# A hybrid attention block on one core: forget gates' sums by a recurrence on VectorE, projection products placed between a linear head's levels, other queue orders at the two norms

## The chip, the core and the metric

The kernel runs on one core of one Trainium2 chip. Five engines work side by side, each through its own queue in order: TensorE (PE, matrix products and transpositions), VectorE (DVE), ScalarE (ACT, activation functions and copies), GpSimd (POOL) and SyncE (SP, which here only issues transfers). Waits between them go by semaphores. The metric is the device time of one execution in microseconds (us); the time before is a median of 937.77 us over three runs, 936.5 to 938.24.

## What is computed

One layer over 512 tokens of width 1024, with 16 learned meta tokens ahead of them (T = 528) that are dropped at the end. The input is normed and projected to all parts; a stick-breaking attention (8 heads of 64) and a gated linear attention (GLA, 4 heads, key width 128, value width 256) run on the same normed tokens; sigmoid gates merge them, `w_o` projects back, and after a second norm a gated MLP (width 2816) with a causal convolution follows. The change lies mostly in the linear attention and in the two norms. Cut to that, the reference is:

```python
h = rmsnorm(concat([meta, x]), norm_mix_pre)
... = split(h @ w_in)                        # sb q,k,v; gla q,k,v; r; lr (16 wide); gates
g = log_sigmoid(lr @ w_gk_up + b_gk) / 16    # log forget gate, per token and key channel
# GLA, per head, S: 128 x 256
S_t = diag(exp(g_t)) S_{t-1} + k_t^T v_t
o_t = q_t S_t
gla = rmsnorm_per_head(o) * silu(r)
```

The kernel works in chunks of 128 tokens. With `cum` the running sum of g inside a chunk, a pair of tokens t > s in one chunk has the weight (q_t exp(cum_t)) . (k_s exp(-cum_s)). So that no exponential overflows, the pairs are dealt out to levels 64, 32, 16, 8, 4, 2 and 1: at level l, block after block of 2l tokens, the later half is taken against the earlier, with `cum` counted from the last token of the earlier half.

## The kernel before

Numbers are float32. A product is made as three products in the faster type fp32r: an operand is split into a high part (a cast on ACT) and a low part (a subtraction on DVE or POOL), and high x high, high x low and low x high are added in PSUM.

**Weights.** `load_w` (L78 to L91) fetches a block of 128 columns as `raw_x` by a transfer that SP issues, casts it to `wh_x` on ACT (L88) and subtracts on POOL (or DVE) to `wl_x` (L89). There are three raw buffers and two of each part. In the names, gk, gq, gv, gr are the linear heads' key, query, value and output gate, sk, sq, sv the attention's, mg and ms the merging gates', ga and up the MLP's.

**Projections.** `proj` (L100, products at L115) makes `pt_x` (128 columns x 528 tokens, or 514 for gr): for each of eight input blocks three products, each over two segments of tokens (272 and 256), 48 products in all. It issues them in one go; where they land on TensorE is chosen by the scheduler, which orders each engine's queue from the order of the program and its own estimates of time, with `tc.issue_after` as a means to hold an instruction behind another.

**First norm** (L214 to L300). Tokens come as four tiles of 128 (`xt`) and the meta tokens (`xm`). Each is squared and summed on ACT, scaled, transposed on TensorE (`tp`, `tpm`), multiplied by the gain on DVE (`yg`, `ygm`, L210), and split into `hnh` (ACT, L211) and `hnl` (DVE or POOL, L212). TensorE's first projection products, `pt_gk` of head 0 over the first 272 tokens, need tiles 1 and 2 and the meta tokens.

**Forget gates** (L367 to L409). The low-rank projection `lr` (16 wide) is made for all tokens, then for each chunk one product `pg` (L402) gives 128 tokens x 512 channels. The bias, spread over 128 partitions by its own transfer (`bbc`), is added on DVE, and Abs, Exp and Ln on ACT give the log sigmoid in `G`, tokens on the partitions.

**A linear head** (`gla`, L436). It is called for four heads. First five fp32 products of `G` with a triangle of 1/16, `ucum`, sum the gates and turn them (`cum`, L440: 10 rows in the profile), and ACT copies the result. Then come the near blocks of 32 (`dg`, L451), the factors of each level on DVE and ACT (`factors`, L458), the levels' small products (`pl`, L482 for 64 and 32, L493 for 16 to 1), the transposed values (`vt`, L520) and keys (`kdt`, L541), and the recurrence over chunks (`po` L558, `pu` L565, with splits of the state on DVE). The output is normed, transposed (`ot`, L590), multiplied by the gate that two gr projections give, and split into `oh` and `ol` (L142, L143). The main loop then makes the next head's projections:

```python
kqv = gla_proj(0)
for h in range(GH):
    gla(h, *kqv)
    kqv = gla_proj(h + 1) if h + 1 < GH else sb_proj(0)
```

All projections of gr and of the next head are thus free work that the scheduler places where TensorE would wait.

**End of the last linear head.** `sb_proj(0)` (L336) makes the first pair of attention heads; `sb_parts` (L612) splits keys and queries into `ks`, `qh` and `ql` on ACT and DVE, transposes the values (`svt`), and the logits of the 16 meta tokens (`zs`, L640) are the first products that need them. The second pair's projections (`pt_sk`, `pt_sq`) and then the merging gates' (mg) follow as free work; with two buffers, `wh_mg` takes the one that the products of `pt_sq` leave.

**Second norm** (L863 to L1010). `w_o`'s products, then per tile of 128 tokens: `hb` (residual), a square on ACT (`wk`, L883), the root (`r_ffn`, Ln at L124 and Exp at L125), `y` on DVE (L888), a transposition (`ht`, L897), and the split into `h2h` and `h2l`. The first products of the MLP (`pt_up`, `ga`) fill in between tiles 3 and 4; `wh_ga` are two blocks of its weights.

Of the kernel before, what the change touches and what calls it, by code (L numbers as in the profile page):

```python
# [39 lines left out]
C_MSB, C_MGLA = 4624, 5648  # L40
CHUNKS = [(0, 128), (128, 128), (256, 128), (384, 128), (512, 16)]
WARM = 6
EASY = 4
EARLY = 3
# [5 lines left out]
def block_kernel(ctx: ExitStack, tc: tile.TileContext, x, meta_tokens, norm_mix_pre, w_in, w_gk_up, b_gk,  # L50
# [22 lines left out]
    def f32(ap):  # L73
        return ap.bitcast(F32)
# [4 lines left out]
    def load_w(src, nk, name, hi_out=None, lo_out=None, lo_eng=pool, into=None):  # L79
# [8 lines left out]
        act.copy(hi_out, raw)  # L88
        lo_eng.tensor_tensor(out=lo_out, in0=raw, in1=f32(hi_out), op=ALU.subtract)  # L89
# [10 lines left out]
    def proj(w, xh, xl, segs, name, apart=False, only=None, pt=None, by_part=False):  # L100
# [11 lines left out]
        for grp in ([[s] for s in segs] if apart else [segs]):  # L112
            for n, (k, a, b) in enumerate(steps):
                for dst, lo, hi in grp:
                    last_pr[0] = pe.matmul(dst, a[:, k, :], b[:, k, lo:hi], start=n == 0, stop=n == len(steps) - 1)  # L115
        return pt if begins else pt[:m, 512 - l1 + l0 : 512 + l2 - l1]

    last_exp = [None]

    def rstd_of(pl, ss, n, name, between=None, rest=None):  # L120
# [15 lines left out]
        dve.scalar_tensor_tensor(out=a, in0=a, scalar=1.5, in1=r0, op0=ALU.add, op1=ALU.mult)  # L136
# [3 lines left out]

    def split(hi, lo, src):
        act.copy(hi, src)  # L142
        last_low[0] = dve.tensor_tensor(out=lo, in0=src, in1=f32(hi), op=ALU.subtract)  # L143
# [36 lines left out]
    ucum = cst.tile([P, P], F32, name="ucum")  # L180
# [6 lines left out]
    pool.memset(ucum, 1.0 / 16.0)  # L187
    pool.affine_select(out=ucum, in_=ucum, compare_op=ALU.is_ge, fill=0.0, base=0, pattern=[[1, P]], channel_multiplier=-1)
# [12 lines left out]
    g2T = cst.tile([P, KT], F32, name="g2T")  # L201
    mT = cst.tile([P, NM - T0, KT], F32, name="mT")
# [4 lines left out]
    def split_g(pl, hi, lo, src, g, nm, lo_eng=dve):  # L207
# [3 lines left out]
        last_hi[0] = act.copy(hi, y)  # L211
        return lo_eng.tensor_tensor(out=lo, in0=y, in1=f32(hi), op=ALU.subtract)  # L212

    with tc.tile_pool(name="p0", bufs=2, side="right") as p0:  # L214
# [37 lines left out]
        def scaled(xt, r, eng):  # L252

            if eng is act:
                act.mul(xt, xt, r)
            else:
                eng.tensor_scalar(out=xt, in0=xt, scalar1=r, scalar2=None, op0=ALU.mult)

        def turned(i, r):
            if not i:  # L260
                tp = pst("tpm")
                last_tp[0] = pe.transpose(tp[:, :P], xm, ident)
                split_g(p0, hnh[:, :, :NM], hnl[:, :, :NM], tp[:, :P].rearrange("p (t k) -> p k t", k=KT), gT, "m")
                return
            t = slice(NM + (i - 1) * P, NM + i * P)
            for b in range(2):
                scaled(xts[i][:, 512 * b : 512 * b + 512], r, SC[i][b])
            for b in range(2):
                tp = pst(f"tp{i}_{b}", "sz"[i % 2])
                for k in range(4):  # L270
                    c = (4 * b + k) * P
                    with tc.issue_after(last_pr[0].ins) if i > 2 else ExitStack():
                        last_tp[0] = pe.transpose(tp[:, k * P : (k + 1) * P], xts[i][:, c : c + P], ident)
                ks = slice(4 * b, 4 * b + 4)
                low = split_g(p0, hnh[:, ks, t], hnl[:, ks, t], tp.rearrange("p (k t) -> p k t", k=4), gT[:, ks], f"{i}_{b}", LO[i][b])
            return low
# [3 lines left out]
        LO = {1: (pool, pool), 2: (dve, pool), 3: (dve, pool), 4: (dve, pool)}  # L280
        d1 = stats(1)
        d2 = stats(2, last_exp[0])
        turned(1, d1)
# [9 lines left out]
        turned(0, d0)  # L293
        hi2 = last_hi[0]
# [5 lines left out]
        turned(3, d3)  # L300
        low4 = turned(4, d4)
# [960 lines left out]
```

## Time and profile before

| | |
|---|---|
| three runs, median | 937.77 us (936.5 to 938.24) |
| the profiled execution's own time | 938.61 us |
| its span in the trace | 936.9 us |
| TensorE busy | 915.9 us, 98% |
| VectorE, ScalarE, GpSimd busy | 621.9, 494.2 and 355.6 us |
| mean rate of the transfers | 100 GB/s |

The span is the time between the first and the last instruction of one profiled execution. The columns of a timeline row are start, duration (both in us), engine, line, operation, the tiles written and read, and in brackets the idle time ahead of it and what ended that. A row of the chain of waits is start, duration, engine and line, and the number of instructions. A row of the windows gives the stretch, its length, the busy time of TensorE, its weight loads, DVE, ACT and POOL, then the clock granted to TensorE (1.00 is full), the transfers' share and their rate.

### The profile page before, as it was taken

What the parts mean: (1) busy time and instruction counts of PE and PEld (TensorE: products, weight loads), DVE (VectorE), ACT (ScalarE), POOL (GpSimd) and SP (SyncE); (2) the same over time, 40 slices, a digit from 0 to 9 for tenths busy, and PEclk for the clock granted to TensorE, in tenths of its full rate; (3) what the DMA queues carried; (4) which work ended last, traced back from release to release, by engine and by line L of the source; (5) the groups of instructions that cost most, each with busy time, mean ns of one, the idle gap of its engine ahead of it and who ended that gap; (6) DMA issues with size and microseconds to landing.
All of it is one profiled execution on the core that took longest, in us unless ns stands there. A gap on an engine that the chain in (4) does not pass through costs nothing.

```text
span 936.9 us, 17749 instructions
## 1 busy us (share of the span) xinstructions
PE 915.9 (98%) x7156; PEld 839.4 (90%) x7156; DVE 621.9 (66%) x1072; ACT 494.2 (53%) x938; POOL 355.6 (38%) x259
## 2 busy tenths in 40 slices
PE   7999999999999999999999998999999999999997
PEld 7999999999999998989998687999999999988885
DVE  6585858686559786888647357455554444578997
ACT  7674747575567665766754245433333333355654
POOL 6533332323355453555545322544444444200200
PEclk9999999999999999999999998999999999999999
DMA  7222222222222222222224542333333333264933
GB/s 203 66 70 75 63 68 69 69 69 69 69 68 69 68 66 72 68 69 68 57 79 127 211 135 90 108 96 91 90 91 90 93 100 100 91 232 184 239 113 131
DMA packets 129875, 93.38 MB, mean 100 GB/s; under 512 B 4080, under 2 KB 114930, under 8 KB 129794
## 3 DMA queue, kind: packets, MB, share of 16 engines
q1 hardware_dynamic: 126178, 82.55, 29.6%
q10 hardware_dynamic: 2112, 6.82, 1.9%
q0 software_dynamic: 1504, 2.88, 1.8%
q8 instruction: 56, 0.92, 0.4%
q14 instruction: 25, 0.20, 0.1%
HBM read 88.05 MB, written 4.19 MB: 98 GB/s over the span
## 4 chain that ended last, share of the span: by engine, by line
PE 94%; DVE 2%; ACT 2%; issue 1%; DMA 0%; POOL 0%; DVEq 0%; POOLq 0%; ACTq 0%
PE pt_up L115 14%; PE ga L936 13%; PE pt_gr L115 5%; PE pt_gv L115 5%; PE pt_mg L115 5%; PE pt_ms L115 5%; PE pt_go L115 5%; PE dA L1108 3%; PE dB L1108 3%; PE dD L1108 3%; PE pt_sv L115 3%; PE pt_gk L115 3%; PE pt_so L115 3%; PE wob L951 3%; PE pt_sk L115 3%; PE pt_gq L115 2%
## 5 line engine op out<-in xcount | busy, mean ns | idle before, releaser
L89 POOL TENSOR_TENSOR wl_up<-raw_up,wh_up 128x1024 fp32r<-128x1024 f32 x22 | 52.9, 2407 | 82.4 <-ACT wh_up L88 82.4
L89 POOL TENSOR_TENSOR wl_ga<-raw_ga,wh_ga 128x1024 fp32r<-128x1024 f32 x22 | 55.3, 2518 | 74.8 <-ACT wh_ga L88 57.5
L115 PE MATMUL pt_up<-h2h,wh_up 128*128 128x256 f32 (+1 forms) x352 | 74.7, 287 | 1.3 <-ACT h2h L142 1.3
L115 PE MATMUL pt_up<-h2l,wh_up 128*128 128x256 f32 (+1 forms) x352 | 74.6, 286 | 0.0
L115 PE MATMUL pt_up<-h2h,wl_up 128*128 128x256 f32 (+1 forms) x352 | 74.4, 285 | 0.0
L936 PE MATMUL ga<-h2h,wh_ga 128*128 128x512 f32 (+1 forms) x192 | 72.5, 377 | 0.0
L936 PE MATMUL ga<-h2h,wl_ga 128*128 128x512 f32 (+1 forms) x192 | 72.3, 377 | 0.0
L936 PE MATMUL ga<-h2l,wh_ga 128*128 128x512 f32 (+1 forms) x192 | 72.3, 377 | 0.0
L88 ACT CAST wh_up<-raw_up 128x1024 fp32r<-128x1024 f32 x22 | 23.1, 1049 | 79.3 <-PE pt_up L115 76.4
L115 PEld LDWEIGHTS pt_up<-h2h,wh_up 128*128 128x128 f32 x352 | 58.0, 193 | 3.5 <-ACT h2h L142 1.8
L115 PEld LDWEIGHTS pt_up<-h2l,wh_up 128*128 128x128 f32 x352 | 56.6, 193 | 0.0
L115 PEld LDWEIGHTS pt_up<-h2h,wl_up 128*128 128x128 f32 x352 | 56.5, 192 | 0.0
L936 PEld LDWEIGHTS ga<-h2h,wl_ga 128*128 128x128 f32 x192 | 36.4, 190 | 7.0
L936 PEld LDWEIGHTS ga<-h2h,wh_ga 128*128 128x128 f32 x192 | 36.7, 191 | 6.1
L936 PEld LDWEIGHTS ga<-h2l,wh_ga 128*128 128x128 f32 x192 | 36.4, 190 | 6.2
L1039 DVE SCALAR_TENSOR_TENSOR cy<-pt_up,cw,cy 128x511 f32<-128x511 f32 (+1 forms) x22 | 16.4, 745 | 36.7 <-ACT cy L1036 36.7
L88 ACT CAST wh_ga<-raw_ga 128x1024 fp32r<-128x1024 f32 x22 | 23.1, 1048 | 26.8 <-PE ga L936 25.6
L1039 DVE SCALAR_TENSOR_TENSOR yp<-pt_up,cw,yp 128x511 f32<-128x511 f32 (+1 forms) x22 | 16.4, 745 | 30.9 <-ACT yp L1036 30.9
L1136 POOL DMA_DIRECT2D tv<-in_w_ffn_down_dram x6 | 7.0, 1172 | 68.4 <-DVE wl_p L143 68.4
L89 POOL TENSOR_TENSOR wl_gr<-raw_gr,wh_gr 128x1024 fp32r<-128x1024 f32 x8 | 19.1, 2385 | 31.0 <-ACT wh_gr L88 29.5
L142 ACT CAST sh_p<-As 128x512 fp32r<-128x512 f32 (+1 forms) x30 | 17.3, 584 | 23.9 <-PE dB L1108 9.6
L115 PE MATMUL pt_gr<-hnh,wh_gr 128*128 128x258 f32 (+1 forms) x128 | 28.2, 294 | 0.0
(574 smaller groups left out, 3140.9 us busy)
## 6 DMA issues: line engine op xcount, KB each, us to landing
raw_up<-in_w_ffn_up_dram SPq DMA_DIRECT2D x22, 512.0 KB, 3.9
raw_ga<-in_w_ffn_gate_dram SPq DMA_DIRECT2D x22, 512.0 KB, 3.8
raw_t<-in_w_ffn_down_dram SPq DMA_DIRECT2D x10, 512.0 KB, 7.4
raw_gv<-in_w_in_dram SPq DMA_DIRECT2D x8, 512.0 KB, 3.9
raw_gr<-in_w_in_dram SPq DMA_DIRECT2D x8, 512.0 KB, 3.8
raw_mg<-in_w_in_dram SPq DMA_DIRECT2D x8, 512.0 KB, 3.9
raw_go<-in_w_gla_out_dram SPq DMA_DIRECT2D x8, 512.0 KB, 4.2
raw_ms<-in_w_in_dram SPq DMA_DIRECT2D x8, 512.0 KB, 3.8
```

The source lines that it names most:

```text
L88: act.copy(hi_out, raw)
L89: lo_eng.tensor_tensor(out=lo_out, in0=raw, in1=f32(hi_out), op=ALU.subtract)
L115: last_pr[0] = pe.matmul(dst, a[:, k, :], b[:, k, lo:hi], start=n == 0, stop=n == len(steps) - 1)
L142: act.copy(hi, src)
L936: last_mm[0] = pe.matmul(pt[:, lo:hi], a[:, k, :], b[:, k, lo:hi], start=lo == 0 and k == 0 and q == 0, stop=k == KT - 1 and q == 2, skip_ ...
L951: last_mm[0] = pe.matmul(pt, a, b, start=q == 0, stop=q == len(ops) - 1)
L1039: dve.scalar_tensor_tensor(out=y[:, d:], in0=pt[:, : SEQ - d], scalar=c, in1=y[:, d:], op0=ALU.mult, op1=ALU.add)
L1108: mm[i] = pe.matmul(dsts[i], a, b, start=first and k == 0 and j == 0, stop=last and k == NP - 1 and j == 2, skip_group_check=True)
L1136: return lambda n, q, nk: pool.dma_start(out=t[:, q : q + nk, :], in_=block(s, c, q, nk), accum_op=ALU.add)
```

## The change

**Sums of the gates.** The gates are made channels on the partitions: for each head two products `pg` over 272 and 256 tokens, with the bias (`bT`, 128 x 4, loaded small and turned with other constants) in ACT's Abs and in a DVE add-and-minimum. A recurrence on DVE (`tensor_tensor_scan`: state = begins x state + gate, `begins` 0 at each chunk's start) writes `cums` for all four heads ahead of head 0. `ucum`, the `cum` products and their copies, `G` and the load of `bbc` are gone; the factor 1/16 goes into the scale of each Exp.

**Products between the levels.** `proj` becomes a generator, `proj_steps`, that yields after each pair of products. `gla` is handed the next head's projections as a generator (`ahead`), chains them behind its own two gr projections, and takes 6, 9, 6, 6 or 8 steps at five kinds of places (`FILL`): behind the near blocks, ahead of each level, ahead of `kdt`, ahead of each `po`, and ahead of `ot`. What is left is issued at the end of the head.

**Queue orders.** At the first norm the scaling of the meta tokens, the first weights' subtraction and several splits are held behind other instructions. At the second norm, tile 3's splits are held behind tile 4's second square, and the second gate block's cast behind tile 2's split.

```diff
+FILL = (6, 9, 6, 6, 8)
...
+    def proj_steps(w, xh, xl, segs, name, apart=False, only=None, pt=None, by_part=False):
...
                 for dst, lo, hi in grp:
                     last_pr[0] = pe.matmul(dst, a[:, k, :], b[:, k, lo:hi], start=n == 0, stop=n == len(steps) - 1)
+                yield
...
-        scaled(xm, d0, act)
-        low2 = turned(2, d2)
-        with tc.issue_after(last_exp[0].ins), tc.issue_after(last_yg[0].ins):
-            first = {"k": load_w(cols(w_in, C_GK), KT, "gk0", lo_eng=dve)}
+        t2 = turned(2, d2)
+        with tc.issue_after(last_exp[0].ins):
+            raw, *first["k"] = load_w(cols(w_in, C_GK), KT, "gk0", lo_eng=None)
+        xs = scaled(xm, d0, act)
...
+        with tc.issue_after(xs.ins):
+            parted(1, 1, t1[1])
+        with tc.issue_after(xs.ins):
+            low20 = parted(2, 0, t2[0])
...
+        with tc.issue_after(last_yg[0].ins):
+            low = dve.tensor_tensor(out=first["k"][1], in0=raw, in1=f32(first["k"][0]), op=ALU.subtract)
+        with tc.issue_after(low.ins):
+            low20()
+            lowm()
...
+            for h in range(GH):
...
+                for (lo, hi), tag in zip(ALL, "sz"):
+                    pc = pst(f"pg{h}{tag}", tag)[:, : hi - lo]
+                    pe.matmul(pc, wg[:, h * P : (h + 1) * P], gst[:, lo:hi], start=True, stop=True)
+                    act.activation(e[:, lo:hi], pc, AF.Abs, bias=bias)
+                    dve.tensor_scalar(out=m[:, lo:hi], in0=pc, scalar1=bias, scalar2=0.0, op0=ALU.add, op1=ALU.min)
+                act.activation(e, e, AF.Exp, scale=-1.0)
+                act.activation(e, e, AF.Ln, bias=1.0)
+                dve.tensor_tensor(out=m, in0=m, in1=e, op=ALU.subtract)
+                dve.tensor_tensor_scan(out=cums[:, h, :], data0=begins, data1=m, initial=0.0, op0=ALU.mult, op1=ALU.add)
...
-        def gla(h, k, q, vT):
-
-            pt = mmt(f"cum{h}")
-            for c, (t, n) in enumerate(CHUNKS):
-                pe.matmul(pt[:, t : t + n], G[:n, c, h * P : (h + 1) * P], ucum[:n, :n], start=True, stop=True)
-            cum = pg.tile([P, T], F32, tag="cum", name=f"cum{h}", bufs=1)
-            act.copy(cum, pt[:, :T])
+        def gla(h, k, q, vT, ahead):
...
+                return (yield from ahead)
+
+            it = between()
+
+            def fill(n):
+                for _ in range(n):
+                    next(it)
+
+            cum = cums[:, h, :]
...
                 pl = pst(f"pl{h}_{lv}", "z")
+                fill(FILL[1])
...
             for c, (t, n) in enumerate(CHUNKS):
                 po = pst(f"po{h}_{c}")
+                fill(FILL[3])
...
+            kqv = gla(h, *kqv, gla_proj(h + 1) if h + 1 < GH else sb_proj(0))
...
-            split(h2h[:, ks, t], h2l[:, ks, t], tp.rearrange("p (k t) -> p k t", k=4))
+            with tc.issue_after(last_wk[0].ins) if i == 3 else ExitStack():
+                split(h2h[:, ks, t], h2l[:, ks, t], tp.rearrange("p (k t) -> p k t", k=4))
...
-        gas = [load_w(cols(w_gate, m * P), KT, f"ga{m}", into=wx) for m in range(2)]
+        gas = [load_w(cols(w_gate, 0), KT, "ga0", into=wx)]
+        with tc.issue_after(parts2.ins):
+            gas.append(load_w(cols(w_gate, P), KT, "ga1", into=wx))
```

The scheduler makes the queues anew from this. Three places show it. On TensorE, around levels 16 and 8 of the second head (`pl_16`, `pl_8`; `pt_gr` is the head's output gate), there stands before:

```order
L115 MATMUL pt_gr_1836<-hnh,wl_gr_1833 128x256
L115 MATMUL pt_gr_1836<-hnh,wh_gr_1832 128x258
L493 MATMUL pl_16_1491<-qt_16_1488,kt_503 32x16 x16
L493 MATMUL pl_8_1516<-qt_8_1513,kt_504 32x16 x16
L493 MATMUL pl_8_1516<-qt_8_1513,kt_504 16x8
L115 MATMUL pt_gr_1836<-hnh,wh_gr_1832 128x256
```

and after, around level 16:

```order
L131 MATMUL pt_gr_1561<-hnh,wl_gr_1558 128x258
L131 MATMUL pt_gr_1561<-hnh,wl_gr_1558 128x256
L556 MATMUL pl_16_1546<-qt_16_1543,kt_518 32x16 x16
L131 MATMUL pt_gr_1561<-hnh,wh_gr_1557 128x258
L131 MATMUL pt_gr_1561<-hnh,wh_gr_1557 128x256
L131 MATMUL pt_gr_1561<-hnl,wh_gr_1557 128x258
L131 MATMUL pt_gr_1561<-hnl,wh_gr_1557 128x256
```

The two levels stood in a row; now 18 products lie between level 16 and level 8, and as many or 12 between the others.

On DVE at the first norm (`yg` and `ygm` are the tiles and the meta tokens after the gain, `a_in` a step of the root, `wl_gk` the first weights' low part, `hnl` the low parts), before:

```order
L210 TENSOR_TENSOR yg_0_193<-tp_0_188,gT 128x512
L132 TENSOR_SCALAR a_in_182<-v_in_180,r_in_177 128x1
L210 TENSOR_TENSOR yg_1_202<-tp_1_197,gT 128x512
L136 SCALAR_TENSOR_TENSOR a_in_182<-a_in_182,r_in_177 128x1
L89 TENSOR_TENSOR wl_gk_209<-raw_gk_206,wh_gk_208 128x1024
L212 TENSOR_TENSOR hnl<-yg_0_193,hnh 128x4x128
L210 TENSOR_TENSOR ygm<-tpm,gT 128x128
L212 TENSOR_TENSOR hnl<-ygm,hnh 128x8x16
```

and after:

```order
L228 TENSOR_TENSOR yg_0_203<-tp_0_181,gT 128x512
L150 TENSOR_SCALAR a_in_176<-v_in_174,r_in_171 128x1
L154 SCALAR_TENSOR_TENSOR a_in_176<-a_in_176,r_in_171 128x1
L228 TENSOR_TENSOR yg_1_206<-tp_1_186,gT 128x512
L228 TENSOR_TENSOR ygm<-tpm,gT 128x128
L322 TENSOR_TENSOR wl_gk_194<-raw_gk_191,wh_gk_193 128x1024
L231 TENSOR_TENSOR hnl<-yg_0_203,hnh 128x4x128
L231 TENSOR_TENSOR hnl<-ygm,hnh 128x8x16
```

The meta tokens' gain stood behind the weights' low part and a tile's; now it stands ahead of both. On ACT the scaling of the meta tokens, before behind three casts of `hnh`, now stands ahead of them.

On ACT at the end of the last linear head, before:

```order
L142 CAST oh<-gated_2_3355 128x2x256
L88 CAST wh_sv_3968<-raw_sv_3966 128x1024
L142 CAST oh<-gated_4_3362 128x2x16
L620 CAST ks_3548<-raw_k_3366 64x528
L624 ACTIVATE qh_3549<-raw_q_3423 64x528
```

some steps of the same kind on, `wh_mg` came behind the casts of `qh` and a copy:

```order
L142 CAST vs_3563<-svt_0_3564 128x8x64
L142 CAST vs_3563<-svt_4_3571 16x2x64
L626 CAST qh_3549<-qh_3549 64x528 x2
L340 COPY raw_k_3851<-pt_sk_3858 128x528
L88 CAST wh_mg_4024<-raw_mg_4022 128x1024
```

and after:

```order
L91 CAST wh_sv_3951<-raw_sv_3949 128x1024
L162 CAST oh<-gated_0_3485 128x2x242
L162 CAST oh<-gated_2_3494 128x2x256
L162 CAST oh<-gated_4_3501 128x2x16
L91 CAST wh_mg_4007<-raw_mg_4005 128x1024
L679 CAST ks_3531<-raw_k_3102 64x528
L683 ACTIVATE qh_3532<-raw_q_3275 64x528
```

`wh_mg` has moved from behind the attention's parts to ahead of them. On TensorE at the same place, 59 products of the second pair (11 of `pt_sk`, 48 of `pt_sq`) and the value transpositions `svt` stood between the last `ot` and `zs` before; now it is 17 of `pt_sq` and `svt`, and the other 42 products lie ahead of the last `ot`.

More of the change, by code (lines that the diff above doesn't have):

```diff
@@ L98, in block_kernel, with drained, proj @@
     last_pr = [None]
-    def proj(w, xh, xl, segs, name, apart=False, only=None, pt=None, by_part=False):
+    def drained(it):
+        while True:
+            try:
+                next(it)
+            except StopIteration as end:
+                return end.value
+    def proj(*a, **k):
+        return drained(proj_steps(*a, **k))
+    def proj_steps(w, xh, xl, segs, name, apart=False, only=None, pt=None, by_part=False):
         wh, wl = w
@@ L211, in split_g @@
         last_hi[0] = act.copy(hi, y)
+        if lo_eng is None:
+            return lambda: dve.tensor_tensor(out=lo, in0=y, in1=f32(hi), op=ALU.subtract)
         return lo_eng.tensor_tensor(out=lo, in0=y, in1=f32(hi), op=ALU.subtract)
@@ L254, in scaled @@
             if eng is act:
-                act.mul(xt, xt, r)
-            else:
-                eng.tensor_scalar(out=xt, in0=xt, scalar1=r, scalar2=None, op0=ALU.mult)
+                return act.mul(xt, xt, r)
+            return eng.tensor_scalar(out=xt, in0=xt, scalar1=r, scalar2=None, op0=ALU.mult)
         def turned(i, r):
[L260 to L265, printed above, removed]
             for b in range(2):
                 scaled(xts[i][:, 512 * b : 512 * b + 512], r, SC[i][b])
+            tps = []
             for b in range(2):
-                tp = pst(f"tp{i}_{b}", "sz"[i % 2])
+                tps.append(pst(f"tp{i}_{b}", "sz"[i % 2]))
                 for k in range(4):
@@ L272, in turned @@
                     with tc.issue_after(last_pr[0].ins) if i > 2 else ExitStack():
[L273 to L276, printed above, removed]
+                        last_tp[0] = pe.transpose(tps[b][:, k * P : (k + 1) * P], xts[i][:, c : c + P], ident)
@@ new lines, in block_kernel @@
+        xs = scaled(xm, d0, act)
+        tp = pst("tpm", "z")
+        last_tp[0] = pe.transpose(tp[:, :P], xm, ident)
+        with tc.issue_after(xs.ins):
+            parted(1, 1, t1[1])
+        with tc.issue_after(xs.ins):
+            low20 = parted(2, 0, t2[0])
+        with tc.issue_after(r0.ins):
+            parted(2, 1, t2[1])
+        with tc.issue_after(last_yg[0].ins):
+            lowm = split_g(p0, hnh[:, :, :NM], hnl[:, :, :NM], tp[:, :P].rearrange("p (t k) -> p k t", k=KT), gT, "m", None)
@@ L339, in sb_proj @@
             t = pst_.tile([P, T], F32, tag=nm, name=f"raw_{nm}{j}")
-            act.copy(t, proj(load_w(cols(w_in, c0 + j * P), KT, f"s{nm}{j}"), hnh, hnl, ALL, f"s{nm}{j}"))
+            pt = yield from proj_steps(load_w(cols(w_in, c0 + j * P), KT, f"s{nm}{j}"), hnh, hnl, ALL, f"s{nm}{j}")
+            act.copy(t, pt)
             r.append(t)
@@ L419, in gla_proj @@
                 else:
-                    with tc.issue_after(first["lr"].ins) if h == 0 else ExitStack():
-                        pt = proj(w, hnh, hnl, ALL, f"g{nm}{h}", apart=h == 0)
+                    steps = proj_steps(w, hnh, hnl, ALL, f"g{nm}{h}", apart=h == 0)
+                    if h == 0:
+                        with tc.issue_after(first["lr"].ins):
+                            pt = drained(steps)
+                    else:
+                        pt = yield from steps
                 t = pgc.tile([P, T], F32, tag=f"g{nm}", name=f"g{nm}{h}", bufs=2)
```

103 lines of the change are left out of this document (59 added, 44 removed).

## The prediction

> **What bounds the kernel now.** I read the page first, then TensorE's waits, then the chain of waits and the timelines at the three places where TensorE stands. The page gives the span, the engines' busy time and the chain that ended last:
>
> ```profile
> span 936.9 us, 17749 instructions
> PE 915.9 (98%) x7156; PEld 839.4 (90%) x7156; DVE 621.9 (66%) x1072; ACT 494.2 (53%) x938; POOL 355.6 (38%) x259
> PE 94%; DVE 2%; ACT 2%; issue 1%; DMA 0%; POOL 0%; DVEq 0%; POOLq 0%; ACTq 0%
> ```
>
> TensorE is busy for 98% of the span and is 94% of the chain; all the rest together is some 21 us. So the change can gain in two ways: fewer or denser TensorE instructions, or shorter waits of TensorE. The longest waits are these (us in total, times, longest):
>
> ```profile
> PE ht L897 <- DVE y L888: 2.6, 1, 2.6
> PE pt_up L115 <- ACT h2h L142: 1.3, 1, 1.3
> PE zs L640 <- ACT qh L626: 0.9, 1, 0.9
> ```
>
> The first two are the second norm, the third is the end of the last linear head, where attention begins. The first norm is read in its own part.
>
> **The sums leave TensorE.** These are rows of the chain (start, us, line, products): the first and the last of four `cum` groups, one per head, and a long run of projection products.
>
> ```profile
> 39.95 7.46 PE pt_gv L115 x61
> 47.41 1.21 PE cum L440 x10
> 191.73 1.21 PE cum L440 x10
> ```
>
> All four `cum` groups stand on the chain, nothing runs beside them on TensorE, and the products of the next stage move up. Their removal is worth 4 x 1.21 = **-4.8 us**. A projection product costs 7.46 / 61 = 0.122 us. What takes their place is four scans on DVE, all made ahead of head 0. No row shows a scan. Eight gate products go with them, in place of five:
>
> ```profile
> L402 PE MATMUL pg<-wg,gst 128*128 128x512 f32 x4 | 1.3, 394 | 0.0
> ```
>
> 512 columns cost 1.3 / 4 = 0.33 us here; before there are 5 x 512 = 2560 columns, after 4 x (272 + 256) = 2112, so 448 x 0.33 / 512 = 0.29 less. Three more groups begin, so I take **-0.2 us**. The scans are needed only by head 0's first level at about 48 us; the gates stood ready by 47.4 before, and DVE is busy for 66%. Bounds: 0, and 0.7 us for each scan that is not covered (an elementwise DVE instruction over 528 columns, a row below), 2.8 us at the very worst; I take 0, since head 0's key, query and value products lie between and cover it. The bias broadcast goes from SP's queue, a small load takes its place and gq's weights are issued one place later; gq's products wait for the low-rank products anyway, so nothing is put down for them.
>
> **Products between the levels.** Head 1's levels in the chain:
>
> ```profile
> 102.68 0.98 PE pl L482 x24
> 103.66 3.07 PE pt_gr L115 x24
> 106.73 0.68 PE pl L493 x53
> 110.36 0.45 PE pl L493 x33
> 114.30 0.40 PE pl L493 x33
> ```
>
> There is hardly an idle stretch here to be filled: the groups already follow on products. Levels 64 and 32, and 16 and 8, stand in pairs (0.98 and 0.68), level 1 alone (0.40). After, each level stands alone with 12 to 18 products on either side. The pair 16 and 8 would cost 2 x 0.40 = 0.80 instead of 0.68, that is 0.12 per second entry. The 24 products behind the wide pair took 3.07 where 24 x 0.122 = 2.93 were due, so a return costs 0.14. A separated pair thus costs 0.26; two are separated per head. Levels 4 and 2 stand apart already (0.45 for the first), 0 to 0.1. The near blocks, which followed on `cum`, now stand among products too: 0.12. That is 2 x 0.26 + 0.12 = 0.64 a head, **+2.5 us** for four, with 1.0 (only the entries count) and 3.5 as ends.
>
> Weights: a tile of eight steps feeds 48 products, 5.9 us, and its successor needs a cast (1.05 us) and a low part on POOL (2.38 us, both rows below) with two buffers. More work now stands ahead of the casts on ACT at times; I put **+0.3 us** for all heads, ends 0 and 1.5.
>
> **The first norm.** ACT, PE, DVE and POOL rows of the timeline (start, us), and the window's row (TensorE busy, loads, DVE, ACT, POOL, granted clock, DMA, GB/s):
>
> ```profile
> 10.05 1.03 ACT L88 CAST wh_gk<-raw_gk 128x1024 fp32r<-128x1024 f32 x1
> 12.55 0.40 ACT L255 ACTIVATE xm<-xm,a_in 128x128 f32<-128x128 f32 x1
> 13.00 0.33 PE L262 MATMUL tpm<-ident,xm 128*128 128x128 f32 x1 [2.24 <-ACT xm L255]
> 11.68 3.82 POOL L212 TENSOR_TENSOR hnl<-yg,hnh 128x512 fp32r<-128x512 f32 x2 [0.28 <-ACT hnh L211]
> 12.61 1.76 DVE L212 TENSOR_TENSOR hnl<-yg,hnh 128x512 fp32r<-128x512 f32 x1
> 14.93 0.72 DVE L212 TENSOR_TENSOR hnl<-ygm,hnh 128x128 fp32r<-128x128 f32 x1 [0.36 <-ACT hnh L211]
> 14.95 2.18 PE L115 MATMUL pt_gk<-hnh,wh_gk 128*128 128x272 f32 x8
> 18.13 1.17 PE L115 MATMUL pt_gk<-hnl,wh_gk 128*128 128x272 f32 x8
> 13.95:17.36 3.41, 3.41 (x17) 3.38 (x16) 2.23 (x7) 2.70 (x6) 1.55 (x1) 0.50 0.98 236
> ```
>
> The scaling of the meta tokens waits on ACT behind three casts. Now it stands right behind the cast of the first weights (10.05 + 1.03 = 11.08), so about 1.45 us earlier, and with it the transposition (13.00 to 11.55) and the start of the first products (14.95 to about 13.5). But their last third needs the low part of the meta tokens, ready at 15.65 now. After, the weights' low part (1.2 us) stands ahead of it on DVE, beside the same POOL subtractions, so I put it at 16.75; 8 products of 0.125 behind it end at 17.75 instead of 19.1 to 19.3. That is **-1.4 us**. It supposes that the window of 13.95 to 17.36, which ran at half the clock, no longer does, since TensorE idles less ahead of it; the low part binds all the same. Ends: -0.8, where the window stays halved, and -2.5, where the low part is not late and the 3.41 / 2 = 1.7 of the half clock is won too.
>
> **The second norm.** ACT's rows and the one DVE row that TensorE waits for:
>
> ```profile
> 563.34 1.03 ACT L88 CAST wh_ga<-raw_ga 128x1024 fp32r<-128x1024 f32 x1
> 564.28 0.59 ACT L142 CAST h2h<-ht 128x512 fp32r<-128x512 f32 x1
> 580.00 0.59 ACT L142 CAST h2h<-ht 128x512 fp32r<-128x512 f32 x1
> 580.48 0.21 ACT L125 ACTIVATE r_ffn<-r_ffn 128x1 f32<-128x1 f32 x1
> 581.71 1.41 DVE L888 SCALAR_TENSOR_TENSOR y<-hb,a_ffn,g2bc 128x512 f32<-128x512 f32 x2
> ```
>
> The cast of the second gate weights moves behind tile 2's casts, which come 564.28 - 563.34 = 0.94 us earlier; so does TensorE, which was idle for 1.3. Behind that the end is set by tile 4's `y`: its second square is no longer behind tile 3's first cast, but the logarithm of its root, before ahead of tile 3's second cast (580.00), now stands behind that cast, where only the exponential (580.48) stood. 24 gate products still lie ahead of that cast's transposition, so without an earlier TensorE it stays at 580.00 and `y` comes about 0.5 later (logarithm and one more exponential, 0.2 to 0.3 each). With the 0.94 and a half-clock window less (1.7), 2.6 would be won. Ends +0.5 and -2.6; I take half of the gain, **-1.3 us**, since the moved weights' POOL subtraction falls on tile 3's own sums.
>
> **The end of the last linear head.** PE, ACT, DVE and POOL, then the two clock windows:
>
> ```profile
> 234.29 1.03 PE L590 MATMUL ot<-ident,ob 128*128 128x128 f32 x8
> 238.06 0.29 PE L590 MATMUL ot<-ident,ob 16*128 16x16 f32 x2
> 247.16 0.18 PE L640 MATMUL zs<-qh,ks 128*16 128x16 f32 x1 [0.86 <-ACT qh L626]
> 243.32 0.63 ACT L620 CAST ks<-raw_k 64x528 fp32r<-64x528 f32 x1 [2.43 <-DVE ol L143]
> 246.48 1.28 ACT L626 CAST qh<-qh 64x528 fp32r<-64x528 f32 x2
> 248.28 1.05 ACT L88 CAST wh_mg<-raw_mg 128x1024 fp32r<-128x1024 f32 x1
> 240.93 2.36 DVE L143 TENSOR_TENSOR ol<-gated,oh 128x32 fp32r<-128x32 f32 x1 [1.54 <-ACT oh L142]
> 243.99 0.70 DVE L623 TENSOR_TENSOR ks<-raw_k,ks 64x528 fp32r<-64x528 f32 x1 [0.70 <-ACT ks L620]
> 240.86 2.38 POOL L89 TENSOR_TENSOR wl_sv<-raw_sv,wh_sv 128x1024 fp32r<-128x1024 f32 x1 [4.75 <-ACT wh_sv L88]
> 246.05:249.47 3.42, 2.30 (x20) 1.80 (x19) 2.55 (x6) 3.35 (x7) 0.06 (x1) 1.00 0.12 35
> 249.47:252.88 3.41, 3.41 (x19) 3.34 (x18) 0.11 (x1) 1.74 (x7) 2.30 (x1) 0.50 0.01 2
> ```
>
> From the transposition at 234.29 the logits come at +12.87. From `ot_4` (+3.8) to them lay 59 products and the value transpositions, which cover all but 1.1 us. After, 42 of these (5.1 us) have been used up between the levels, and 17 are left: TensorE is through at +3.8 + 0.3 + 17 x 0.122 + 0.3 = +6.5. On ACT `wh_mg` now stands ahead of `ks`, and it needs the buffer that the last of the 17 products frees: +6.1, so `ks` begins at +7.2. From `ks` to the logits took 247.16 - 243.32 = 3.8: +11.0. POOL's low part starts as soon as `wh_mg` is there; if it holds `ks`'s low part on DVE back to 7.25 + 2.4 = +9.65 (the row of `ol` shows that: 2.36 us for 128x32 elements, ended 0.05 after POOL's subtraction), the logits come 247.16 - 243.99 = 3.2 later less 0.5 of slack: +12.3. TensorE idles 4.5 to 5.8 us, 3.4 to 4.7 more than before. `wh_mg`'s 1.05 no longer lies behind the logits on ACT, where the next wait gets it back: +2.3 to +3.7, **+3.0 us**. The half clock behind it is there already.
>
> On the clock: the window 246.05 to 249.47 had TensorE busy for 2.30 of 3.42 us, and the next ran at 0.50; so an idle 1.1 us was enough. The Trainium skill, "TensorE: Matmul & The Clock Gate", section "What's actually happening", lets a free-running window of 3413 ns throttle only after a whole idle one; the length agrees with the rows, the condition is stricter than the row. By the page the 5.8 us of idle would contain such a window in about 7 of 10 positions (an estimate: (5.8 - 3.41) / 3.41), and 0.3 x 1.7 = 0.5 us would come off the sum.
>
> **The sum.** -4.8 - 0.2 + 2.5 + 0.3 - 1.4 - 1.3 + 3.0 = **-1.9 us**. The profiled execution took 938.61 us beside its span of 936.9; the median of the runs lies 0.84 below it, at 937.77. So 936.7 beside the profile, **935.9 us** as a median. A measurement of this kernel can tell about 0.2%, 1.9 us, from no change: 935.9 lies at that edge.
>
> **Rivals.**
> A, the forecast: 934.3 to 937.4, by the ends of the norms and of the head's end. **0.48**, about half of it on each side of the edge.
> B, the head's end stays covered: `ks` doesn't wait for `wh_mg` because the last products are through before `oh` is cast, and the attention's own products fill in. Then the +3.0 goes: 937.77 - 4.9 = **932.9**. For it: TensorE waited only 1.1 us there. Against it: the 17 products. **0.24**.
> C, slower: at the head's end, `wh_mg` on ACT, then POOL's subtraction on `ks`. No wait gets the 1.05 back, and the longer gap halves one more window: 4.7 + 1.7 = 6.4, with weights late in the levels 1.5: 7.9. All the other terms save 5.2, so it is slower from 5.2, and by over 0.2% from 7.1 on: 937.77 + 2.7 = **940.5**. For it speak the 2.36 us of `ol`; against it, that ACT was idle for 2.43 us ahead of `ks` before. **0.18**. The Trainium skill, "SBUF — State Buffer", section "SBUF: two separate sides", describes a lock of the ports that DVE and GpSimd share, held for the whole instruction, which agrees with the 2.36 us.
> D, the norms give nothing: the low parts at the start and tile 4's sums set the end as before. -2.5 + 3.3 = +0.8, **938.5**. **0.10**.
>
> Faster by over 0.2%: half of A (0.26) and B, 0.50; within 0.2%: 0.22 and D, 0.32; slower: C, 0.18. The range reaches from B less 0.9 for its level term (932.0) to C: 932.0 to 940.5.
>
> **What would show it.** In the profile after: no `cum`; small groups of 0.40 each and products between at 0.122; the first products at about 13.5 with no half-clock window ahead of 17.4; TensorE's wait ahead of `zs` 4.5 to 5.8 us, ended by ACT's `qh` or DVE's `ks`; `y` of tile 4 about 1.3 us nearer to the levels' end than before. The prediction would be wrong if level groups in the midst of products cost 0.2 or 1.0 instead of 0.40, if new waits for weights (`gr`, `gv`) run to over 0.5 us a head, or if the wait ahead of `zs` is under 2 us.

## The result, and the profile after

The changed kernel takes 947.39 us (median of four runs, 946.36 to 949.73) against 938.0 us in the runs beside it: a ratio of 1.010, with a 95% interval of 1.0086 to 1.0115. It is slower by about 9.4 us where 2 us of gain were forecast, and lies outside the range. The page of the profiled execution (one of 949.73 us):

```profile
span 948.0 us, 17647 instructions
PE 918.5 (97%) x7120; PEld 838.0 (88%) x7120; DVE 643.2 (68%) x1079; ACT 492.2 (52%) x935; POOL 354.0 (37%) x260
PE 77%; DVE 11%; ACT 5%; issue 4%; DMA 2%; POOL 0%; SPq 0%; DVEq 0%; ACTq 0%; POOLq 0%
```

TensorE was 94% of the chain before and is 77% now; DVE went from 2% to 11%. TensorE's waits (us in total, times, longest) say where:

```profile
PE zs L699 <- DVE ql L684: 4.1, 1, 4.1
PE ht L957 <- DVE y L948: 3.4, 1, 3.4
PE z L722 <- DVE v0l L167: 2.5, 2, 1.4
PE po L623 <- DVE ob L625: 2.3, 3, 0.8
PE lr L432 <- DVE hnl L232: 1.4, 1, 1.4
PE vt L583 <- DVE vl L163: 1.1, 1, 1.1
PE zs L699 <- DVE ql L686: 1.0, 1, 1.0
PE po L623 <- DVE vl L163: 0.6, 1, 0.6
PE pt_up L131 <- ACT h2h L162: 0.4, 1, 0.4
```

`po` and `vt`, the recurrence inside a linear head, had no wait worth a row before; now they wait five times, 4.0 us in all. `zs` waited 0.9 and waits 5.1 now; `z`, the attention's products behind it, waited 2.4 and waits 2.5. To see what each place cost, the span is cut at three marks that all kernels share: the end of the low-rank products `lr`, the first `zs`, and the first `mini` product of the second norm (from the trace, us):

| kernel (profiled) | to the end of `lr` | to `zs` | to `mini` | to the end | median, ratio to before with interval |
|---|---|---|---|---|---|
| before | 29.0 | 218.1 | 311.9 | 377.9 | |
| after | 32.0 | 224.4 | 313.8 | 377.8 | 947.39, 1.010 (1.0086 to 1.0115) |
| sums alone | 30.7 | 217.1 | 310.7 | 377.6 | 936.05, 0.9971 (0.9961 to 0.9981) |
| placement alone | 31.8 | 222.6 | 313.1 | 374.1 | 941.34, 1.0034 (1.002 to 1.0049) |
| sums and placement | 30.0 | 224.4 | 313.4 | 374.1 | 943.58, 1.005 (1.0035 to 1.0065) |
| after, factors held | 30.7 | 217.6 | 319.5 | 376.0 | 943.25, 1.0045 (1.0026 to 1.0064) |
| after, gv low parts on DVE | 31.0 | 219.3 | 316.6 | 376.0 | 944.56, 1.0071 (1.0045 to 1.0096) |
| after, mg late | 30.7 | 223.4 | 311.6 | 377.1 | 944.15, 1.007 (1.0052 to 1.0087) |
| after, first norm of before | 29.1 | 224.3 | 313.0 | 376.9 | 945.45, 1.0085 (1.0066 to 1.0104) |
| after, gq low part on DVE | 31.2 | 221.7 | 313.4 | 377.1 | 944.84, 1.0062 (1.0037 to 1.0087) |
| after, second norm of before | 33.7 | 224.4 | 312.9 | 375.0 | 945.69, 1.0087 (1.0065 to 1.0109) |
| best parts, placement in three heads | 30.8 | 213.4 | 319.5 | 375.9 | 940.21, 1.0004 (0.9982 to 1.0025) |
| sums, factors and second norm held | 29.2 | 215.8 | 310.5 | 377.8 | 935.24, 0.996 (0.9945 to 0.9974) |
| sums, factors held | 29.0 | 215.7 | 310.6 | 378.1 | 934.93, 0.9954 (0.9936 to 0.9972) |

Below the row of after, the ratios are to runs of before beside each kernel, with medians of 938.7 to 939.1 us instead of 938.0; so a difference between two medians of the table is uncertain by about 1 us.

The 11.1 us between the two spans are +3.0 at the start, +6.3 in the linear heads and their end, +1.9 behind that, and -0.1 for all the rest.

### The profile page after: what moved, and what is told of

The parts are those of the page before. It is cut to its first block, busy times and chain, and to the rows that moved or that the text cites. A ratio compares the mean times of both kernels' runs of the same rounds, so it can differ in the third digit from the quotient of the medians.

```text
span 948.0 us, 17647 instructions
## 1 busy us (share of the span) xinstructions
PE 918.5 (97%) x7120; PEld 838.0 (88%) x7120; DVE 643.2 (68%) x1079; ACT 492.2 (52%) x935; POOL 354.0 (37%) x260
## 4 chain that ended last, share of the span: by engine, by line
PE 77%; DVE 11%; ACT 5%; issue 4%; DMA 2%; POOL 0%; SPq 0%; DVEq 0%; ACTq 0%; POOLq 0%
PE pt_up L131 13%; PE ga L997 13%; PE pt_mg L131 5%; PE pt_ms L131 5%; PE pt_go L131 4%; PE dD L1173 3%; PE dB L1173 3%; PE pt_sv L131 3%; PE pt_gr L131 3%; PE pt_sk L131 3%; PE wo L1033 2%; PE wob L1012 2%; PE dA L1173 2%; PE pt_sq L131 2%; PE pt_gv L131 2%
```

## Experiments: the linear heads

**The theory**: with all sums made ahead, and the next head's key and query products drawn ahead between the levels, the next head's level factors become free early. They move on VectorE ahead of this head's own outputs, run there beside GpSimd's subtraction of weights, and are held by it. **The rival**: the many small groups of products cost TensorE more than was reckoned.

Three kernels have the recurrence alone, the placement alone, and both, all with the norms of before. The first takes the placement out of the kernel after (`fill` leads nowhere, gr is issued ahead of `ot`, the next head's projections behind it):

```diff
-                return (yield from ahead)
...
-            fill(FILL[4])
+            drained(it)
...
-            return drained(it)
+            return drained(ahead)
```

The second keeps the placement and puts `cum`, `G` and `bbc` back:

```diff
-            cum = cums[:, h, :]
+            pt = mmt(f"cum{h}")
...
+                pe.matmul(pt[:, t : t + n], G[:n, c, h * P : (h + 1) * P], ucum[:n, :n], start=True, stop=True)
```

> The kernel before with the recurrence alone: gates as after, no products placed between levels, both norms as before. Theory (the sums made ahead let the next head's level factors run early on VectorE, ahead of the head's own outputs and beside GpSimd's weight subtractions, and that makes the new waits of about 4 us in the four heads): four cum groups gone (-4.8) and -0.2 in the gates, less some of the new waits since the next head's factors do stand earlier here too: 933 to 937 against 938.0, waits of po or vt for VectorE over 0.3 us in the trace. Rival (the placement alone makes the waits): 933.0 and no such wait.

> The kernel before with the placement alone: cum products on TensorE as before, products between the levels and the last head's end as after, both norms as before. Theory: levels +2.5, the end of the last head +4.1 and the second half-clock window behind it +1.8, and no waits of po for VectorE, since the next head's factors wait for its own cum: 938.0 + 8.4 = 946.4. Rival (the placement makes the waits of po): 4 more, 950.

> The kernel after with both norms as before. Theory: the start's loss of 3.1 us is due to the new order of the first norm, the second norm's order was worth nothing: 947.4 - 3.1 = 944.3, and the first tokens' key and low-rank products end as before. Rival (the start is late because of the gates' new form and not the norm's order): 947.4.

A row of the trace that needs no choice measures three heads: the first and the last start of `kdt`, which comes once a head (x16 is four heads of four). Before:

```profile
L541 PE MATMUL kdt<-ident,kd x16: 272/273/331, 69.9 to 214.9; 128*128 128x128 f32 x16
```

the sums alone:

```profile
L580 PE MATMUL kdt<-ident,kd x16: 270/273/328, 73.0 to 214.0; 128*128 128x128 f32 x16
```

the placement alone:

```profile
L591 PE MATMUL kdt<-ident,kd x16: 270/272/273, 78.5 to 224.0; 128*128 128x128 f32 x16
```

both:

```profile
L589 PE MATMUL kdt<-ident,kd x16: 272/273/331, 76.8 to 224.0; 128*128 128x128 f32 x16
```

The differences of the last two numbers are 145.0, 141.0, 145.5 and 147.2 us. The stretches don't hold quite the same work: counted in the traces, 863 to 865 projection products lie in three of them and 840 in that of the sums alone, whose other 25 come later. At 0.122 us each that is 3.0 us. So of the 4.0 that the sums alone seem to win 1.0 is left: their `cum` products are gone, but TensorE now waits 3.3 us in these heads for the levels' factors and for `kdt`, where before it waited 0.4. The placement alone costs 0.5. Together they cost 2.2, and 2.7 more than the two add up to.

Neither part is slow by itself: the rival falls, and so does the first half of my expectation for the sums alone, that waits of `po` would show there without the placement. The trace of the sums alone has none; those waits need both. The placement alone was expected at 946.4 and took 941.34: its levels cost less than I reckoned, and its second norm, with the code of before, took 374.1 us instead of 377.9 (below).

Then the held kernel: after, with only the first level's factors of the next head behind this head's last output on VectorE.

```diff
+                with tc.issue_after(last_ob[0].ins) if h and lv == WIDE[0] else ExitStack():
-                dve.tensor_tensor(out=dv, in0=cv, in1=cv[:, :, lv - 1 : lv].broadcast_to([P, nb, 2 * lv]), op=ALU.subtract)
+                    dve.tensor_tensor(out=dv, in0=cv, in1=cv[:, :, lv - 1 : lv].broadcast_to([P, nb, 2 * lv]), op=ALU.subtract)
```

> The kernel after with the first level's factors of the next head held behind the last copy of this head's output on VectorE. Theory: the waits of po and vt for VectorE (4.1 us in all) go, and nothing new waits since 30 products lie ahead of the first level: 947.4 - 3.5 = 943.9. Rival (the waits come from the products' place on TensorE, or VectorE is just full): waits stay or move to pl, 947.4 or more.

After, and the held kernel:

```profile
L605 PE MATMUL kdt<-ident,kd x16: 272/273/328, 78.8 to 226.0; 128*128 128x128 f32 x16
L608 PE MATMUL kdt<-ident,kd x16: 272/273/328, 76.9 to 217.9; 128*128 128x128 f32 x16
```

Three heads take 141.0 us with the same 864 products, 6.2 less than after, and the waits of `po` go. That is more than the 2.7, since here the placed products cover what the sums alone leave open. TensorE's waits make about half of the 6.2; the rest lies in denser products, whose order the scheduler changed as well, and wasn't taken apart. 943.25 us is what was expected, though not for all its reasons: behind the heads 5.6 us were lost again in the attention (below).

Last, the lock itself. In the kernel after, first GpSimd's row, then two of VectorE's, in the first head:

```profile
84.83 2.40 POOL L94 TENSOR_TENSOR wl_gv<-raw_gv,wh_gv 128x1024 fp32r<-128x1024 f32 x1 [2.51 <-PE pu L630]
...
85.29 2.56 DVE L533 TENSOR_TENSOR qt<-gq,D 128x256 f32<-128x256 f32 x2 [1.02 <-ACT gq L469]
87.77 0.41 DVE L625 COPY ob<-po 128x256 f32<-128x256 f32 x1
```

Two `qt` of the next head need 2.56 us and end 0.6 behind GpSimd's subtraction; `ob`, for whose copy the next `po` waits, stands behind them. Now the low parts of gv on VectorE instead, with `kt` and `qt` ahead of `ob` as in after:

```diff
-lo_eng=pool if h or u else dve)
+lo_eng=dve)
```

> The kernel after with the low parts of the value weights (gv) of all heads on VectorE instead of GpSimd; order otherwise as after. Theory (GpSimd's subtraction holds a VectorE instruction with two operands in SBUF, kt and qt of the next head at 2.2 to 2.5 us): kt and qt take 0.4 each, VectorE pays 1.2 for each of two low parts a head instead, and the four waits of vt and po in the recurrences shrink from 4.1 to under 2.5 us: 947.4 - 1.5 = 945.9. Rival (VectorE is simply full there): it gets 2.4 us a head more to do, and the waits grow: 949 or more.

```profile
82.14 1.23 DVE L94 TENSOR_TENSOR wl_gv<-raw_gv,wh_gv 128x1024 fp32r<-128x1024 f32 x1 [0.52 <-ACT wh_gv L91]
83.28 0.76 DVE L533 TENSOR_TENSOR qt<-gq,D 128x256 f32<-128x256 f32 x2
83.95 0.42 DVE L625 COPY ob<-po 128x256 f32<-128x256 f32 x1
```

```profile
L605 PE MATMUL kdt<-ident,kd x16: 272/273/328, 77.3 to 219.8; 128*128 128x128 f32 x16
```

VectorE does more work and the two `qt` take 0.76; the waits of `po` and `vt`, 4.0 us, fall to 0.2, and three heads take 142.5 us, 4.7 less than after. So the lock is shown to make most of the loss, and VectorE was not full.

## Experiments: the end of the last head

In the kernel after: GpSimd, ScalarE and VectorE, then windows of the clock (their columns as before).

```profile
252.73 2.35 POOL L94 TENSOR_TENSOR wl_mg<-raw_mg,wh_mg 128x1024 fp32r<-128x1024 f32 x1 [4.72 <-ACT wh_mg L91]
...
251.61 1.05 ACT L91 CAST wh_mg<-raw_mg 128x1024 fp32r<-128x1024 f32 x1 [0.35 <-PE pt_sq L131]
252.56 0.63 ACT L679 CAST ks<-raw_k 64x528 fp32r<-64x528 f32 x1
...
253.22 2.42 DVE L682 TENSOR_TENSOR ks<-raw_k,ks 64x528 fp32r<-64x528 f32 x1 [1.74 <-ACT ks L679]
```

```profile
250.29:253.71 3.42, 2.03 (x18) 1.74 (x16) 1.29 (x4) 2.32 (x4) 0.98 (x1) 1.00 0.30 88
253.71:257.12 3.41, 0.18 (x1) 0.09 (x1) 3.33 (x3) 3.19 (x7) 1.37 (x1) 1.00 0.25 71
257.12:260.53 3.41, 2.91 (x16) 2.91 (x17) 2.44 (x5) 1.20 (x2) 0.00 (x0) 0.50 0.28 82
260.53:263.95 3.42, 3.42 (x20) 3.34 (x18) 0.00 (x0) 0.80 (x4) 0.00 (x0) 0.50 0.00 0
```

It went as the prediction worked out: `wh_mg` when the last product leaves its buffer, `ks` behind it, and `ks`'s low part held to 255.6, 0.6 behind GpSimd's end. In the next kernel only `wh_mg`'s cast goes back behind the casts of `qh`:

```diff
-        act.copy(hi_out, raw)
+        with tc.issue_after(after.ins) if after else ExitStack():
+            act.copy(hi_out, raw)
...
-KT, f"mg{j}"), hnh, hnl, LATE, f"mg{j}")
+KT, f"mg{j}", after=last_q0 if j == 0 else None), hnh, hnl, LATE, f"mg{j}")
```

> The kernel after with one cast moved: the merging gate's first weights behind the attention's casts of qh, as before. Theory (their cast on ScalarE and GpSimd's low part hold the attention's parts back at the last head's end): the parts begin 0.95 earlier and the low part of ks is not blocked for 1.7 us, TensorE's wait ahead of zs falls from 5.1 to 2.5 us and one of two half-clock windows goes: 947.4 - 2.6 - 1.7 = 943.1. Rival (17 products are too little cover whatever the weights do): the wait stays over 4 us, 947.

```profile
250.93 0.70 DVE L684 TENSOR_TENSOR ks<-raw_k,ks 64x528 fp32r<-64x528 f32 x1 [0.75 <-ACT ks L681]
```

The low part takes 0.70 instead of 2.42, and the wait falls from 5.1 to 3.7 us, not to 2.5; the rest is the missing cover, and both half-clock windows stay. The gain of 3.2 us in the medians isn't all the cast's: by the table 1.0 is in the stage to `zs` and 2.2 behind it, where the wait of `z` falls from 2.5 to 1.0; and the profiled start ended 1.3 earlier, where this edit has no part. Theory and rival are each half right.

## Experiments: the two norms

The start of the kernel after: GpSimd, VectorE and ScalarE, the low-rank products on TensorE, and the window:

```profile
18.37 2.67 POOL L94 TENSOR_TENSOR wl_gq<-raw_gq,wh_gq 128x1024 fp32r<-128x1024 f32 x1 [0.49 <-ACT wh_gq L91]
...
19.26 0.69 DVE L228 TENSOR_TENSOR yg<-tp,gT 128x512 f32<-128x512 f32 x1
19.87 1.19 DVE L154 SCALAR_TENSOR_TENSOR a_in<-a_in,r_in 128x1 f32<-128x1 f32 x1
...
21.09 1.34 ACT L275 ACTIVATE xt<-xt,a_in 128x512 f32<-128x512 f32 x2 [0.49 <-DVE a_in L154]
...
28.65 0.45 PE L432 MATMUL lr<-hnl,wst 128*48 128x256 f32 x1 [1.36 <-DVE hnl L232]
```

```profile
25.01:28.43 3.42, 2.28 (x22) 1.90 (x20) 3.31 (x5) 0.38 (x2) 3.06 (x6) 1.00 0.01 2
28.43:31.84 3.41, 3.19 (x15) 2.96 (x16) 1.64 (x9) 0.00 (x0) 1.47 (x3) 0.50 0.00 0
```

The last step of tile 4's root, one column, takes 1.19 us: it now stands behind a gain (19.26), and so falls under GpSimd's subtraction, which ends at 21.04. Before, it was over at 18.85, ahead of that subtraction. Tile 4's scaling, transposition and low part follow, TensorE runs out of products 1.36 us ahead of `lr`, and then half the clock covers all of `lr`'s second part. Three runs belong to this. The first norm of before, put into the kernel after:

```diff
-        for i, d in ((3, d3), (4, d4)):
-            for b, tp in enumerate(turned(i, d)):
-                low4 = parted(i, b, tp)
+        turned(3, d3)
+        low4 = turned(4, d4)
...
```

> The kernel after with the first norm's order of before; the second norm stays as after. Theory (in the new order tile 4's root stands behind a gain on VectorE and runs into GpSimd's subtraction of gq's low part, so its low parts and the low-rank products are late, 3.0 us at their end): the low-rank products end at 30 us instead of 32.0, 947.4 - 2.0 = 945.4. Rival (the start is late by the gates' new form): 947.4, the same end.

The low-rank products end at 29.1 instead of 32.0, and the median is 945.45, 1.9 less, though the intervals of the two ratios overlap. Now the low part of gq on VectorE:

```diff
-first["q"] = load_w(cols(w_in, C_GQ), KT, "gq0")
+first["q"] = load_w(cols(w_in, C_GQ), KT, "gq0", lo_eng=dve)
```

> The kernel after with the low part of the first query weights (gq of head 0) on VectorE instead of GpSimd. Theory (that subtraction holds the last step of tile 4's root for 1.0 us at the start): the step takes 0.15 to 0.3 instead of 1.19, tile 4's scaling begins about 1 us earlier; VectorE pays 1.2 for the low part, so the low-rank products end at 31 to 32 instead of 32.0: 946.5 to 947.4. Rival (tile 4 is late because of the order on VectorE alone): the step's time falls no more than 0.2.

```profile
19.48 0.15 DVE L154 SCALAR_TENSOR_TENSOR a_in<-a_in,r_in 128x1 f32<-128x1 f32 x1
```

Still behind a gain, the step takes 0.15: the lock is what held it. `lr` ends at 31.2, but by then 71 projection products are done instead of 52, and the wait of 1.36 us ahead of `lr` is gone; the first `zs` comes at 252.8 instead of 256.4. The median is 944.84, 2.6 less, where at most 0.9 was expected. So with the new order kept, taking the lock away wins as much as the old order does.

The end of `lr` itself moves from profile to profile: in five profiles of kernels with the new order it came between 30.7 and 33.7 (mean 31.6), in eight with the old one between 29.0 and 31.8 (mean 30.0). So the order costs 1.6 us on the mean, and 3.0 between the two profiles that are compared here.

The second norm of before in the kernel after:

```diff
-            with tc.issue_after(last_wk[0].ins) if i == 3 else ExitStack():
-                split(h2h[:, ks, t], h2l[:, ks, t], tp.rearrange("p (k t) -> p k t", k=4))
+            split(h2h[:, ks, t], h2l[:, ks, t], tp.rearrange("p (k t) -> p k t", k=4))
...
```

> The kernel after with the second norm's code of before; the first norm stays as after. Theory (the norm's new order holds tile 3's splits and leaves a wait of 3.4 us for tile 4's y and a second half-clock window; with the code of before the scheduler now places 20 gate products between the transpositions and that wait goes): from the second mini product to the end 374.1 us instead of 377.8, 947.4 - 3.7 = 943.7. Rival (what the norm gained or lost is made up behind it): 947.4.

From `mini` to the end it takes 375.0 instead of 377.8, so 2.8 of the 3.7 that were expected; the median gains 1.7, again with overlapping intervals. What is shown here is the code with the order that the scheduler makes of it: the same code in the kernel before takes 377.9, and beside the placement 374.1, 374.1 and 375.0 in three profiles.

Both norms of before together are the kernel with sums and placement: 943.58 us, 3.8 less than after, and there the intervals lie apart. In the kernel after, two rows of VectorE, then the windows behind; the last two lines are before's windows at half the clock in this stage:

```profile
577.35 2.29 DVE L145 TENSOR_SCALAR v_mix<-mssmix 128x2 f32<-128x2 f32 x1
591.42 1.41 DVE L948 SCALAR_TENSOR_TENSOR y<-hb,a_ffn,g2bc 128x512 f32<-128x512 f32 x2
```

```profile
591.63:595.04 3.41, 2.81 (x12) 2.58 (x13) 2.25 (x6) 1.28 (x3) 0.00 (x0) 0.50 0.00 0
595.04:598.45 3.41, 3.41 (x17) 3.41 (x17) 0.51 (x1) 0.00 (x0) 0.00 (x0) 0.50 0.00 0
```

```profile
566.91:570.32 3.41, 3.41 (x18) 3.41 (x17) 3.31 (x13) 1.72 (x6) 0.32 (x1) 0.50 0.88 249
583.97:587.39 3.42, 3.42 (x17) 3.42 (x18) 1.25 (x2) 0.56 (x1) 0.00 (x0) 0.50 0.03 5
```

Tile 4's `y` comes at 591.42, which is 1.5 us earlier than 581.71 and the 11.2 by which the kernel was late at `mini`. The wait ahead of `pt_up` is 0.9 shorter. But TensorE has less left to do until `y` and waits 3.4 instead of 2.6 for it, and two windows run at half the clock as before, only both behind `y`. In the six profiles with the new order this stage takes 376.0 to 377.8 (mean 376.8), in the three with the old one, order and code, 377.6 to 378.1 (mean 377.8): 1.0 is won on the mean, and nothing in the pair compared. Against the code of before in a kernel with the placement (mean 374.4) the new order loses 2.4.

## Experiments: a faster version

Three kernels put the parts together that won. The first keeps the placement in three heads:

```diff
+                if h < GH - 1:
+                    return (yield from ahead)
...
+                    with tc.issue_after(hold.ins) if hold is not None and not (k or q) else ExitStack():
```

> The recurrence and the placement in the first three heads with the next head's first factors held behind this head's outputs, the last head's products placed as before, both norms' code as before, and in the second norm the second gate block's products held behind tile 3's first transposition. Theory: from before's 938.0, heads 3 x -1.3 and -1.2 for the last, the wait for tile 4's y gone (-3.7): 929.2, with the start's phase of the clock +-1.7. Rival (the gains of single places are taken back by later waits): 935 to 938.

It took 940.21 us, 1.0004 of before (0.9982 to 1.0025): the rival. The heads gave what they should, `zs` coming 2.9 us earlier in the trace than before, but the attention behind lost 7.6. In it, TensorE's wait, GpSimd and VectorE:

```profile
PE po L811 <- DVE w0h L166: 2.0, 1, 2.0
```

```profile
356.45 2.54 POOL L94 TENSOR_TENSOR wl_mg<-raw_mg,wh_mg 128x1024 fp32r<-128x1024 f32 x1 [0.17 <-ACT wh_mg L91]
...
356.67 2.75 DVE L720 TENSOR_TENSOR w<-w,E 128x400 f32<-128x400 f32 x1
```

The same subtraction, elsewhere: 2.0 us, and three windows at half the clock behind it (360.9 to 371.1, 5.1 us). The ten runs lie in two groups, 935.2 to 935.5 and 939.1 to 941.7; that the wait decides between them is read from one trace and wasn't tried. The kernel with held factors and the one with gv's low parts on VectorE show the same wait, with three such windows and one behind it. The other two kernels leave the placement out:

```diff
+                with tc.issue_after(last_ob[0].ins) if h and lv == WIDE[0] else ExitStack():
...
-                return (yield from ahead)
```

> The recurrence without placed products, the next head's first factors held behind this head's outputs, both norms' code as before, the second gate block's products in the second norm held behind tile 3's first transposition. Theory: four cum groups (-4.8) and nothing lost in the heads, a part of the wait for tile 4's y gone (-2): 938.9 - 6.8 = 932. Rival (without the cum group something else, the factors themselves, bounds the levels): 935 to 937 as for the recurrence alone.

> As the kernel ahead of it, without the hold in the second norm. Theory: 938.9 - 4.8 = 934; against the recurrence alone (936.05) the waits of pl and kdt for the factors in heads 1 to 3 go, about 3 us in all, and those of head 0 stay. Rival: 936, waits as for the recurrence alone.

They took 935.24 us (0.996, 0.9945 to 0.9974) and 934.93 us (0.9954, 0.9936 to 0.9972). The second beats both kernels, though not surely the sums alone. The first lies in the rival's range, the second between theory and rival. The row of `kdt` in the second:

```profile
L583 PE MATMUL kdt<-ident,kd x16: 270/272/328, 70.4 to 210.9; 128*128 128x128 f32 x16
```

Three heads take 140.5; head 0 still waits 1.3, 1.6 and 0.7 us for its first levels, with no products there to cover them. The hold in the second norm brought nothing.

## Why the prediction was wrong

**Where the sum went wrong.** The forecast of -1.9 us has +0.8 for the heads and their end, and -2.7 for the norms. Measured with both norms' code as before, the change cost 4.8 (943.58 against 938.74 beside it), although the second norm, whose queues the scheduler made anew, ended 3.8 earlier. The norms' orders cost another 3.8 (by the medians) to 4.6 (by the ratios) instead of winning 2.7. So it failed at two steps: the weights in the heads, and the norms.

**The sums, -4.8 and -0.2: too large a gain.** The `cum` rows are gone as forecast, but alone the sums win 2.7 in the medians (936.05 against 938.74). I took 0 for the scans, since products would cover them. Without the placement, the last scan ends at 51.05, the first level's factors start at 51.16, and TensorE waits 3.5 us for head 0's levels, more than the 2.8 put down as the very worst. In the change itself head 0's levels are covered.

**The levels, +2.5: too large.** The placement alone costs 0.5 in three heads, 0.2 a head instead of 0.64.

**The step that failed first: "Weights ... I put +0.3 us".** I priced GpSimd's low parts only as weights that might be late for TensorE, and the two edits only one by one. What they do together, letting the next head's factors run ahead of this head's outputs and into GpSimd's subtractions, had no term. It costs 6.2 us in three heads, by the held kernel, and 4.7 of these go when only gv's subtractions leave GpSimd. With the factors held, the stage from `lr` to `zs` takes 217.6 us, against 224.4 in after and 218.1 before. The factors' new place stood in VectorE's order; I had followed that order only at the start.

**The first norm, -1.4: +3.0, or +1.6 on the mean.** Its first part came true: the first products start at 13.99 instead of 14.95, their first segment ends 0.9 earlier, and no window there runs at half the clock. I stopped there. Tile 4's root, further on in the same queue, sets the end of the stage, and GpSimd's subtraction held it.

**The last head's end, +3.0: +4.3 and +1.9.** The wait of 5.1 us lies inside the 4.5 to 5.8 that were worked out, by the mechanism named. But the 1.05 that was to come back did not, since the next wait stayed (2.5 us), and the gap halved the clock for two windows, not one. That is rival C's price there, without its late weights.

**The second norm, -1.3: 0, or -1.0 on the mean; +2.4 against the code of before beside the placement.** The 0.94 came, and `y` came 1.5 nearer. The half-clock window that was to go did not, and the wait for `y` grew by 0.9. I had compared with before's order alone; the placement gave the old code a better order as well.

All in all slower had a chance of 0.18, for the lock at one place only, while it sat at three.

**On the clock** I said that an idle 1.1 us was enough. The windows above don't bear that out as a rule: 2.28 us of TensorE's time in one window was followed by half the clock, 2.03 in another by the full one. With two such rows no bound can be given. The Trainium skill ("TensorE: Matmul & The Clock Gate", "What's actually happening") asks for a whole idle window; 253.71 to 257.12, almost all idle and followed by half the clock, agrees with it, 25.01 to 28.43 doesn't.

**On the lock**, the Trainium skill ("SBUF — State Buffer", "SBUF: two separate sides") says that VectorE and GpSimd share a pair of ports: of a GpSimd instruction that reads SBUF and a VectorE one with two operands there (or in a mode that uses both ports), the one that starts first keeps the pair to its end, and the other waits. The runs agree: 2.42 against 0.70, 1.19 against 0.15, and 2.56 against 0.76 us.

## What to carry to other kernels

Price edits together where one makes an operand ready early and another moves the work that used to keep its reader back: look through the queue of the engine that isn't the bound for what now stands ahead of its critical results. Where one engine's long instruction can hold another's, a short step on a critical path is worth following to the instant at which it would meet it. And products that fill a gap of one place are missing at the next, where they were cover. When a stretch between two marks is compared between kernels, count the work in it first.

## What the runs showed of the hardware

A scan along 528 elements took 1.24 to 1.26 us on VectorE, against 0.69 for an elementwise instruction of the same width, and once 3.34, beside a GpSimd subtraction that ended 1.1 us ahead of the scan's end. An instruction with a single operand in SBUF was late beside GpSimd as well: `v_mix`, two columns, took 2.29 us in the second norm, from 577.35 to 579.64 beside a subtraction that ended at 579.61, against 0.17 before. The clock's windows fall at another place in every profile, and the start of kernels that share its code ended up to 3.0 us apart, so such kernels are compared by stages too and not by one profile alone.
